# A transformer trunk with two attention branches: the side work of modulation and weight sums goes to GpSimd alone, low parts of weights and masks to VectorE

## The chip, the cores and the metric

The kernel runs on one core of a Trainium2 chip. The core's engines run side by side, each with its own queue of instructions that it works off in order: TensorE (PE in the profile; its weight loads are PEld), VectorE (DVE), ScalarE (ACT), GpSimd (POOL) and SyncE (SP, which here only issues DMAs). An instruction that waits for another engine or for a DMA holds up everything behind it in its own queue, and nothing else. The metric is the device time of one execution in microseconds (us); lower is better. Times of one kernel are given as the median of several runs.

## What is computed

One layer of a streaming encoder on 1024 positions of width 1024, float32 in and out. Cut to what matters:

```python
cond = silu(c)
mod = cond @ w_ada + b_ada                      # six vectors of 1024: shift, scale, gate, twice
sh1, sc1, g1, sh2, sc2, g2 = split(mod, 6)

h = layer_norm(x) * (1 + sc1) + sh1
q_a, k_a, v_a, f_a, q_c, k_c, v_c, gate_a, gate_c = split(h @ w_in)
o_a = forgetting_attention(q_a, k_a, v_a, f_a + b_f)   # causal, 8 heads of 64, cumulative bias
o_c = chunk_band_attention(q_c, k_c, v_c, rel_bias)    # 8 heads, 64-frame chunks, 8 chunks back
merged = sigmoid(gate_a) * (o_a @ w_br_fox) + sigmoid(gate_c) * (o_c @ w_br_chunk)
x = layer_norm(alpha * x + (1 + g1) * (merged @ w_out), ln1_g, ln1_b)

h = layer_norm(x) * (1 + sc2) + sh2
a, val = split(causal_conv3(h @ w_up))
x = layer_norm(alpha * x + (1 + g2) * ((silu(a) * val) @ w_down), ln2_g, ln2_b)
```

## The kernel before

Every matrix product keeps float32 accuracy by splitting its operands: a tile is copied to a rounded high part (`wh`), and the low part (`wl`) is the tile less its high part. Three matmuls (high by high, high by low, low by high) take the place of one. `split` (L100) does this for weights: the copy on ScalarE (L104), the subtraction on GpSimd (L105). A weight tile is 128 x 1024 numbers, loaded into `ws` by `load_w` (L95) through SyncE's queue; `ws`, `wh` and `wl` have two buffers each.

The program has five stretches: the first norm with the first two modulation vectors, attention (from about 113 us), the merge of the branches with the output product, the up-projection with its convolution, and the down-projection. The two large products of the MLP multiply 2 x 2 blocks by a scheme with seven products in place of eight, for which sums and differences of weight blocks are needed; for 8 column blocks of `w_up` and 11 pairs of rows of `w_down` these are prepared during attention and kept in DRAM (`wd`, `td`).

Attention is where the change is. The main loop (L705 to L750) runs over 8 pairs of heads (`plan`), for each over 8 steps of two 128-query blocks. A step computes the scores of the next step (L460, L461 on TensorE), adds the bias and takes the row's extreme on VectorE (L472), the exponential on ScalarE (L478), transposes the probabilities on TensorE (L512), splits them (L515 on ScalarE, L516 on VectorE) and multiplies by the values (L526; added up in L530 and L531). Beside it the loop advances two generators:

- `stream` (class `Stream`): the products of h with `w_in` for later heads and for the gates (tiles `psq`, `psg`, `psv`; L207 to L209 and L309 to L311). It loads raw weights ahead, splits them, and runs units of matmuls. `step` (L263) issues one piece of a unit and then calls `load` and `split`.
- `side_work` (L533): one step of it for each step of `stream` in the loop. It walks through 35 groups, each with one tile `dr` of 128 x 4 x 512 (two buffers). A sums group loads weight blocks, makes four sums or differences on GpSimd (L584) and stores them to `wd` or `td` (L587). A modulation group (16 of them, between the first sums groups) loads half of the rows of 512 columns of `w_ada` (L553), multiplies each of its four 128 x 512 blocks by a column of `cond` on ScalarE (L571) and adds them into `acc` on GpSimd (L573). After two modulation groups TensorE sums `acc` over the partitions (`ada_sums`, L167), and VectorE adds the bias into `modc` (L161, L163).

All loads and stores of the side work go through SyncE's queue, where the loads of weights, of the heads' biases (`cb` for the chunk branch, `fb` for the other) and the copies of queries and keys (`m`, L407, L408) stand as well. GpSimd also writes two masked corners into each `cb` (L425, L426, after VectorE has scaled it, L424) and adds the causal mask to 64 diagonal blocks `fm` (L438).

The order in which instructions stand in each engine's queue is set when the kernel is built: a list scheduler goes over the program with priorities from the order of the code, so that an edit of one engine's work can shift how the two streams interleave on all engines.

Of the kernel before, what the change touches and what calls it, by code (L numbers as in the profile page):

```python
# [12 lines left out]
F32 = mybir.dt.float32  # L13
F32R = mybir.dt.float32r
AF = mybir.ActivationFunctionType
ALU = mybir.AluOpType
# [3 lines left out]
P = 128  # L20
# [4 lines left out]
H = 512  # L25
# [3 lines left out]
DH = 64  # L29
# [3 lines left out]
NEG = -1e30  # L33
# [10 lines left out]
def body(ctx, tc, a, out):  # L44
    nc = tc.nc
    ve, se, pe, po, sy = nc.vector, nc.scalar, nc.tensor, nc.gpsimd, nc.sync
    uid = [0]

    def nm(s):
        uid[0] += 1  # L50
        return f"{s}_{uid[0]}"

    def opened(**kw):
        cm = tc.tile_pool(reuse_waits="tile", **kw)
        return cm, cm.__enter__()
# [8 lines left out]
    def ctile(name, shape, src=None, dt=F32):  # L64
        t = const.tile(shape, dt, name=name, tag=name)
        if src is not None:
            se.dma_start(out=t, in_=src)
        return t
# [10 lines left out]
    cond = ctile("cond", [P, KD])  # L79
# [17 lines left out]
        sy.dma_start(out=st, in_=src)  # L97
        return st

    def split(st, shape, pool=None):  # L100
        n = 2 if pool is None else 1
        hi = (pool or wp).tile(shape, F32R, name=nm("wh"), tag="wh", bufs=n)
        lo = (pool or wp).tile(shape, F32R, name=nm("wl"), tag="wl", bufs=n)
        se.copy(out=hi, in_=st)  # L104
        po.tensor_sub(out=lo, in0=st, in1=hi)  # L105
        return hi, lo

    def split_w(src, shape, pool=None):
# [39 lines left out]
    def ada_src(v, c0, n):  # L148
        return a["w_ada"][:, v * D + c0 : v * D + c0 + n].rearrange("(k p) n -> p k n", p=P)
# [7 lines left out]
    def ada_bias(ps, v, c0, n, plus_one):  # L157
        sl = slice(v * KD + c0 // P, v * KD + (c0 + n) // P)
        ps = ps[:, 0 : n // P]
        if plus_one:  # L160
            ve.scalar_tensor_tensor(out=modc[:, sl], in0=ps, scalar=1.0, in1=bada[:, sl], op0=ALU.add, op1=ALU.add)  # L161
        else:
            ve.tensor_tensor(out=modc[:, sl], in0=ps, in1=bada[:, sl], op=ALU.add)  # L163

    def ada_sums(ps, acc, n):
        for j in range(n // P):
            pe.matmul(ps[:, j : j + 1], acc[:, j * P : (j + 1) * P], ones[:, 0:1], start=True, stop=True)  # L167
# [54 lines left out]
    pmm = es.enter_context(tc.tile_pool(name="pmm", bufs=3, space=PSUM, reuse_waits="tile"))  # L222
# [7 lines left out]
    class Stream:  # L230


        def __init__(self, units):
            self.units = units
            self.parts = [(u, p) for u in range(len(units)) for p in units[u].parts]
            self.loaded, self.ready, self.live, self.age = [], {}, 0, 0
            self.pl = self.ps = self.cur = 0
            self.gen = None

        def load(self):  # L240
            if self.pl < len(self.parts) and self.pl - self.ps < 2:
                _, (src, shape) = self.parts[self.pl]
                self.loaded.append((load_w(src, shape), shape))
                self.pl += 1
                return True
            return False

        def split(self):
            if self.loaded and self.live < 2:
                u = self.parts[self.ps][0]  # L250
                self.ready.setdefault(u, []).append(split(*self.loaded.pop(0)))
                self.ps += 1
                self.live += 1
                return True
            return False
# [7 lines left out]
        def step(self):  # L263
            unit = self.units[self.cur]
            if self.gen is None:
                self.prime(self.cur)
                self.gen = unit.run(self.ready.pop(self.cur, []))
            cost = next(self.gen, None)
            if cost is None:
                self.live -= len(unit.parts)  # L270
                self.gen = None
                self.cur += 1
                cost = 0.0
                self.load()
            else:
                self.load()
                self.split()
            return cost

        def finish(self, upto):  # L280
# [139 lines left out]
    def scaled():  # L420

        while unscaled:
            b = unscaled.pop(0)
            ve.tensor_scalar_mul(b, b, 1.0 / SCALE)  # L424
            po.memset(b[0:DH, 576:640], NEG)  # L425
            po.memset(b[DH:P, 0:64], NEG)  # L426

    def first_block(br, qi):
        return 0 if br == 0 else max(0, qi - 4)
# [3 lines left out]
    def masked(n, i):  # L433

        (ip, hi, g), qi = steps[n], 2 * steps[n][2] + i
        if ip < 4 and (n, i) not in masks:
            fm = ap.tile([P, P], F32, name=nm("fm"), tag="fm", bufs=4)
            po.tensor_tensor(out=fm, in0=heads[ip, hi][3][:, qi * P : (qi + 1) * P], in1=cmask, op=ALU.add)  # L438
            masks[n, i] = fm
        return masks.get((n, i))  # L440

# [91 lines left out]
    def side_work():  # L533

        sub = ALU.subtract
        ups = ((3, 2, 3, ALU.add), (2, 0, 2, sub), (0, 3, 0, sub), (1, 1, 0, sub))
        downs = ((0, 1, 0, sub), (1, 3, 1, sub), (3, 3, 0, sub), (2, 2, 3, sub))
        sums_ = [(ups, a["w_up"][2 * c : 2 * c + 2].rearrange("b p (j k) n -> p b j (k n)", j=2), wd[c]) for c in range(HEAD)]  # L540
        for i in range(NPAIR):
            srcs = [a["w_down"][order[2 * i + r]].rearrange("p (j n) -> p j n", j=2) for r in range(2)]
            sums_.append((downs, srcs, td[i]))
        vecs = [(v, half, q) for v in (2, 4, 3, 5) for half in range(2) for q in range(2)]
        groups = [g for pair in zip(sums_, vecs) for g in pair] + sums_[len(vecs) :]
        tiles, due = {}, []

        def load(n):
            if n < len(groups):
                x = tiles[n] = ap.tile([P, 4, H], F32, name=nm("dr"), tag="dr", bufs=2)  # L550
                if n % 2 and n < 2 * len(vecs):
                    v, half, q = groups[n]
                    sy.dma_start(out=x, in_=ada_src(v, half * H, H)[:, 4 * q : 4 * q + 4, :])  # L553
                else:
                    srcs = groups[n][1]
                    for r in range(2):
                        sy.dma_start(out=x[:, 2 * r : 2 * r + 2, :], in_=srcs[r] if isinstance(srcs, list) else srcs[:, r])

        load(0)
        yield  # L560
        load(1)
        yield
        for n, group in enumerate(groups):
            x = tiles.pop(n)
            if n % 2 and n < 2 * len(vecs):
                v, half, q = group
                if q == 0:
                    acc = ap.tile([P, H], F32, name=nm("acc"), tag="acc", bufs=1)
                for j in range(4):
                    k = 4 * q + j  # L570
                    se.mul(out=x[:, j, :] if k else acc, in_=x[:, j, :], mul=cond[:, k : k + 1])  # L571
                    if k:
                        po.tensor_tensor(out=acc, in0=acc, in1=x[:, j, :], op=ALU.add)  # L573
                    if j % 2:
                        yield
                if q:
                    ps = pmm.tile([P, H], F32, name=nm("psada"), tag="mm")
                    ada_sums(ps, acc, H)
                    due.append(partial(ada_bias, ps, v, half * H, H, v != 3))
            else:  # L580
                while due:
                    due.pop()()
                for j, (o, p, q, op) in enumerate(group[0]):
                    po.tensor_tensor(out=x[:, o, :], in0=x[:, p, :], in1=x[:, q, :], op=op)  # L584
                    if j % 2:
                        yield
                sy.dma_start(out=group[2].rearrange("j p n -> p j n"), in_=x)  # L587
                yield
                yield
            load(n + 2)  # L590
            yield

# [14 lines left out]
    stream = Stream(first_units + [u for grp in groups for u in grp] + [unit_g()])  # L607
# [29 lines left out]
    cmask = ctile("cmask", [P, P], a["cmask"])  # L637
# [8 lines left out]
    for c in range(4):  # L646
# [4 lines left out]
        for v in (0, 1):  # L651
            if v or row is None:
                acc = s1.tile([P, W], F32, name=nm("acc"), tag=f"acc{v}", bufs=1)
# [7 lines left out]
    for kk in range(2):  # L661
        shape = v_unit.parts[kk][1]
        hi = fp.tile(shape, F32R, name=nm("wh"), tag=f"wh{kk}")
        lo = fp.tile(shape, F32R, name=nm("wl"), tag=f"wl{kk}")
# [18 lines left out]
    f_cm.__exit__(None, None, None)  # L683
    ap_cm, ap = opened(name="attn", bufs=2)

    steps = [(ip, i, g) for ip, _ in plan for i in range(2) for g in range(4)]
    heads = {}

# [16 lines left out]
    for u, (ip, _) in enumerate(plan):  # L705
# [5 lines left out]
        for n in range(8 * u, 8 * u + 8):  # L711
            ip, i, g = steps[n]
# [525 lines left out]
    with tc.tile_pool(name="dn", bufs=2, reuse_waits="tile") as dn:  # L1238
# [44 lines left out]
        for p in products:  # L1283
            ps = bank_b if p in ("P5", "P3", "P2") else bank_a
# [44 lines left out]
            elif p in ("P3", "P2", "P7"):  # L1329
                for t in range(4):  # L1330
                    x = {"P3": u2, "P2": p1, "P7": p5}[p][t]
                    ve.tensor_tensor(out=x, in0=ps[t], in1=x, op=ALU.add)
                    tt, n = {"P3": (t, 1), "P2": (t, 0), "P7": (4 + t, 1)}[p]
# [68 lines left out]
```

## Time and profile before

| What | Before |
|---|---|
| Time, median of 3 runs | 1678.43 us (1678.13 to 1678.95) |
| Profiled execution, its time | 1677.85 us |
| Its span on the chip | 1675.7 us |
| TensorE busy | 1544.7 us, 92% |
| VectorE busy | 1029.6 us, 61% |
| ScalarE busy | 788.1 us, 47% |
| GpSimd busy | 594.4 us, 35% |
| DMA of SyncE's queue (q1) | 251.83 MB |
| DMA of ScalarE's queue (q10) | 19.75 MB |
| DMA of GpSimd's queue (q0) | 1.84 MB |

The profile lists what each engine did and when. A row of a waits view reads: engine, tile and line that waited, what it waited for, the total in us, how many times, the longest. A row of a timeline reads: start in us, duration in us, engine, line, operation, written tile and read tiles, shapes; in square brackets how long the engine had been idle before and what ended that. A row of a windows view gives for a stretch its length and the busy time of PE, PEld, DVE, ACT and POOL, then the share of TensorE's clock that was granted (PEclk), the DMA engines' busy share and GB/s. A row of a groups view gives line, engine, operation, tiles, shapes and count, then busy us and mean ns of one, then the idle time before.

### The profile page before, as it was taken

The page shows a single profiled execution, that of the slowest core. Times are in us where ns is not written, and L with a number is a line of the kernel's source. Part 1 is how long each engine was busy: PE and PEld are TensorE (multiplying, and loading weights), DVE is VectorE, ACT ScalarE, POOL GpSimd, SP SyncE. Part 2 cuts the span into 40 slices and gives each one's busy share as a digit, 9 for nine tenths or more (in the row PEclk, how much of TensorE's full clock was granted, in tenths as well). Part 3 has the DMA queues.
Part 4 walks back from the last instruction along what each step waited for, and adds up shares of the span by engine and source line. Part 5 has one row for each costly group of instructions (what it writes and reads, how often), then busy time and mean ns, then how long its engine had stood idle before and what let it go on. Part 6 is the DMA issues. An engine that isn't in the chain of part 4 may idle for free. (4 is left out here: it accounts for less than half of the span.)

```text
span 1675.7 us, 22014 instructions
## 1 busy us (share of the span) xinstructions
PE 1544.7 (92%) x7693; PEld 1293.0 (77%) x7693; DVE 1029.6 (61%) x2053; ACT 788.1 (47%) x1420; POOL 594.4 (35%) x455
## 2 busy tenths in 40 slices
PE   6899788989998799999889798899999999999996
PEld 3788678879777788888667686688888888888885
DVE  6746344445534435443667968667777866855688
ACT  3447444555535434444223435444445455456451
POOL 1126516435355263212303364554544555100000
PEclk9999999999999899999989899899999999999998
DMA  9037735355274354423763725434344222597552
GB/s 358 26 109 252 235 126 177 117 194 183 84 236 153 101 177 157 133 70 111 225 247 118 261 93 197 156 135 149 119 142 166 101 103 86 177 375 251 181 198 81
DMA packets 118766, 274.81 MB, mean 164 GB/s; under 512 B 11008, under 2 KB 19904, under 8 KB 118656
## 3 DMA queue, kind: packets, MB, share of 16 engines
q1 hardware_dynamic: 106464, 251.83, 44.4%
q10 hardware_dynamic: 11664, 19.75, 3.1%
q0 software_dynamic: 528, 1.84, 0.3%
q8 instruction: 60, 0.98, 0.2%
q14 instruction: 50, 0.41, 0.1%
HBM read 197.51 MB, written 67.47 MB: 158 GB/s over the span
## 5 line engine op out<-in xcount | busy, mean ns | idle before, releaser
L105 POOL TENSOR_TENSOR wl<-ws,wh 128x1024 fp32r<-128x1024 f32 x54 | 131.1, 2433 | 312.6 <-ACT wh L104 283.7
L831 PE MATMUL psu<-hc,wx 128*128 128x512 f32 x720 | 168.4, 389 | 0.0
L831 PEld LDWEIGHTS psu<-hc,wx 128*128 128x128 f32 x720 | 135.1, 188 | 28.1
L1067 DVE SCALAR_TENSOR_TENSOR pcv<-u,convp,pcv 128x1024 f32<-128x1024 f32 x88 | 113.2, 1286 | 45.4 <-ACT pcv L1065 44.4
L1208 DVE TENSOR_TENSOR op<-rw,op 128x512 fp32r<-128x512 f32 x146 | 93.3, 688 | 52.9 <-ACT op L1207 52.4
L1207 ACT CAST op<-rw 128x512 fp32r<-128x512 f32 x146 | 85.2, 623 | 83.5 <-PE psd L1220 41.9
L516 DVE TENSOR_TENSOR pt<-pst,pt 128x512 fp32r<-128x512 f32 (+1 forms) x192 | 96.9, 520 | 36.8 <-ACT pt L515 35.3
L478 ACT ACTIVATE s<-s,mx 128x640 f32<-128x640 f32 (+7 forms) x128 | 94.4, 737 | 45.3 <-DVE mx L472 42.9
L584 POOL TENSOR_TENSOR dr<-dr 128x512 f32<-128x512 f32 x76 | 97.9, 1289 | 47.1 <-DMA dr<-in_w_down 21.9
L1219 PE MATMUL psd<-op,op 128*128 128x512 f32 x292 | 113.7, 389 | 0.9 <-DVE op L1208 0.9
L1218 PE MATMUL psd<-op,op 128*128 128x512 f32 x292 | 113.6, 389 | 0.0
L1220 PE MATMUL psd<-op,op 128*128 128x512 f32 x292 | 113.6, 389 | 0.0
L515 ACT CAST pt<-pst 128x512 fp32r<-128x512 f32 (+1 forms) x192 | 82.5, 450 | 56.4 <-PE pst L512 54.6
L526 PE MATMUL pso<-pt,vs 128*128 128x256 f32 x608 | 92.6, 291 | 17.1 <-ACT pt L515 11.6
L207 PE MATMUL psg<-h1h,wh 128*128 128x512 f32 x256 | 107.0, 418 | 0.0
L209 PE MATMUL psq<-h1h,wl 128*128 128x512 f32 x256 | 102.4, 400 | 4.3 <-POOL wl L105 4.3
L209 PE MATMUL psg<-h1h,wl 128*128 128x512 f32 x256 | 102.6, 401 | 4.0 <-POOL wl L105 4.0
L207 PE MATMUL psq<-h1h,wh 128*128 128x512 f32 x256 | 105.8, 414 | 0.4 <-DVE h1h L203 0.4
L208 PE MATMUL psq<-h1l,wh 128*128 128x512 f32 x256 | 102.5, 400 | 1.8 <-DVE h1l L204 1.8
L526 PEld LDWEIGHTS pso<-pt,vs 128*128 128x128 f32 x608 | 83.7, 194 | 26.1 <-ACT pt L515 15.5
L208 PE MATMUL psg<-h1l,wh 128*128 128x512 f32 x256 | 102.4, 400 | 0.0
L512 PE MATMUL pst<-ident,s 128*128 128x128 f32 x528 | 83.2, 277 | 12.6 <-DVE pt L516 9.7
(261 smaller groups left out, 3939.8 us busy)
## 6 DMA issues: line engine op xcount, KB each, us to landing
ws<-in_w_up SPq DMA_DIRECT2D x36, 512.0 KB, 3.7
dr<-in_w_ada SPq DMA_DIRECT2D x16, 1024.0 KB, 5.4
dr<-in_w_down SPq DMA_DIRECT2D x22, 512.0 KB, 4.5
td<-dr SPq DMA_DIRECT2D x11, 1024.0 KB, 4.6
rw<-td SPq DMA_DIRECT2D x44, 256.0 KB, 4.5
yd<-y SPq DMA_DIRECT2D x20, 512.0 KB, 2.8
rw<-yd SPq DMA_DIRECT2D x40, 256.0 KB, 4.0
rw<-sd SPq DMA_DIRECT2D x33, 256.0 KB, 4.7
```

The costliest lines, as they stand in the source:

```text
L105: po.tensor_sub(out=lo, in0=st, in1=hi)
L207: pe.matmul(ps, wh, xh, start=start, stop=False)
L208: pe.matmul(ps, wh, xl, start=False, stop=False)
L209: pe.matmul(ps, wl, xh, start=False, stop=stop)
L516: ve.tensor_sub(out=dl, in0=src, in1=dh)
L526: pe.matmul(ps[:, 0:256], vs[:, h % 2, j0 + j, :], pt[j // 4][:, c, j % 4, :], start=j == 0 and c == 0, stop=j == nj - 1 and c == 1)
L584: po.tensor_tensor(out=x[:, o, :], in0=x[:, p, :], in1=x[:, q, :], op=op)
L831: pe.matmul(ps, w[:, a_, k, :], h[k][b_], start=first, stop=k == 3 and a_ == 1, skip_group_check=on)
L1067: ve.scalar_tensor_tensor(out=ps, in0=u[b][:, 2 - d : S + 2 - d], scalar=cp[:, 2 - d : 3 - d], in1=ps, op0=ALU.mult, op1=ALU.add)
L1218: pe.matmul(ps[t], g[:, 0, ts], d[:, 0], start=start, stop=False, skip_group_check=on)
L1219: pe.matmul(ps[t], g[:, 0, ts], d[:, 1], start=False, stop=False, skip_group_check=on)
L1220: pe.matmul(ps[t], g[:, 1, ts], d[:, 0], start=False, stop=stop, skip_group_check=on)
```

## The change

- In attention the low parts of the stream's weights are subtracted on VectorE (`stream.eng = ve`); before attention and in the merge they stay on GpSimd. The mask additions (L438) and the two corner memsets go to VectorE too.
- In `side_work` the multiplications by `cond` go from ScalarE to GpSimd, and all its loads and stores from SyncE's queue to GpSimd's own.
- `ada_sums` and the bias are issued later: not straight after the second modulation group, but after the store of the sums group that follows it.
- `Stream.step` calls `load` after `split`, so the next raw weight tile is asked for in the same step as the split that frees its buffer.

```diff
-    def split(st, shape, pool=None):
+    def split(st, shape, pool=None, eng=po):
...
-        po.tensor_sub(out=lo, in0=st, in1=hi)
+        eng.tensor_sub(out=lo, in0=st, in1=hi)
...
-                self.ready.setdefault(u, []).append(split(*self.loaded.pop(0)))
+                self.ready.setdefault(u, []).append(split(*self.loaded.pop(0), eng=self.eng))
...
                 cost = 0.0
-                self.load()
             else:
-                self.load()
                 self.split()
+            self.load()
...
-            po.memset(b[0:DH, 576:640], NEG)
-            po.memset(b[DH:P, 0:64], NEG)
+            ve.memset(b[0:DH, 576:640], NEG)
+            ve.memset(b[DH:P, 0:64], NEG)
...
-            po.tensor_tensor(out=fm, in0=heads[ip, hi][3][:, qi * P : (qi + 1) * P], in1=cmask, op=ALU.add)
+            ve.tensor_tensor(out=fm, in0=heads[ip, hi][3][:, qi * P : (qi + 1) * P], in1=cmask, op=ALU.add)
...
-                    sy.dma_start(out=x, in_=ada_src(v, half * H, H)[:, 4 * q : 4 * q + 4, :])
+                    po.dma_start(out=x, in_=ada_src(v, half * H, H)[:, 4 * q : 4 * q + 4, :])
...
-                        sy.dma_start(out=x[:, 2 * r : 2 * r + 2, :], in_=srcs[r] if isinstance(srcs, list) else srcs[:, r])
+                        po.dma_start(out=x[:, 2 * r : 2 * r + 2, :], in_=srcs[r] if isinstance(srcs, list) else srcs[:, r])
...
         load(0)
+        load(1)
         yield
-        load(1)
         yield
...
-                    se.mul(out=x[:, j, :] if k else acc, in_=x[:, j, :], mul=cond[:, k : k + 1])
+                    po.tensor_scalar_mul(x[:, j, :] if k else acc, x[:, j, :], cond[:, k : k + 1])
...
                 if q:
-                    ps = pmm.tile([P, H], F32, name=nm("psada"), tag="mm")
-                    ada_sums(ps, acc, H)
-                    due.append(partial(ada_bias, ps, v, half * H, H, v != 3))
+                    due.append((acc, v, half))
             else:
-                while due:
-                    due.pop()()
...
-                sy.dma_start(out=group[2].rearrange("j p n -> p j n"), in_=x)
+                po.dma_start(out=group[2].rearrange("j p n -> p j n"), in_=x)
                 yield
-                yield
+                while due:
+                    acc, v, half = due.pop()
+                    ps = pmm.tile([P, H], F32, name=nm("psada"), tag="mm")
+                    ada_sums(ps, acc, H)
+                    yield
+                    ada_bias(ps, v, half * H, H, v != 3)
...
+    stream.eng = ve
```

Three places of the engines' queues, before and after; the line numbers of the changed kernel are 1 or 2 higher in parts. The first is ScalarE's queue beside the values' product of a stream unit (`vs` and `psv`), before the change:

```order
L478 ACTIVATE s_2146,sums<-s_2146,mx_2150 128x384
L314 CAST vs_2163<-psv_2165 128x2x64
L571 ACTIVATE dr_2854<-dr_2854,cond 128x512
L314 CAST vs_2164<-psv_2165 128x2x64
L515 CAST pt_2145<-pst_2203 128x2x128
L571 ACTIVATE dr_2854<-dr_2854,cond 128x512
L478 ACTIVATE s_2196,sums<-s_2196,mx_2200 128x512
```

and the same place of the changed kernel, where the same tiles have other numbers:

```order
L478 ACTIVATE s_2150,sums<-s_2150,mx_2154 128x384
L314 CAST vs_2170<-psv_2172 128x2x64
L515 CAST pt_2149<-pst_2214 128x2x128
L314 CAST vs_2171<-psv_2172 128x2x64
L478 ACTIVATE s_2207,sums<-s_2207,mx_2211 128x512
```

The multiplications of `dr` (L571) are gone from between the copies that attention and the stream wait for. The second place is VectorE's queue at the evacuation of a stream product (`qm` from `psq`), before:

```order
L472 ISA s_1965,mx_1969<-pss_1966,cb_1550 128x384
L472 ISA mx_1969 128x1
L368 TENSOR_TENSOR qm_1789<-psq_1890,qm_1789 64x512
L472 ISA s_1965,mx_1974<-pss_1971,cb_1550,mx_1969 128x256
L472 ISA mx_1974 128x1
```

and in the changed kernel:

```order
L472 ISA s_1973,mx_1977<-pss_1974,cb_1553 128x384
L472 ISA mx_1977 128x1
L105 TENSOR_TENSOR wl_2015<-ws_1646,wh_2014 128x1024
L368 TENSOR_TENSOR qm_1786<-psq_1893,qm_1786 64x512
L472 ISA s_1973,mx_1982<-pss_1979,cb_1553,mx_1977 128x256
L472 ISA mx_1982 128x1
```

A low part now stands between the two halves of a score row. The third place is GpSimd's queue around two modulation groups (`dr_2276` and `dr_2739`) and the sums group between them (`dr_2561`), in the changed kernel alone:

```order
L583 DMA wd<-dr_2130 128x4x512
L571 TENSOR_SCALAR dr_2276<-dr_2276,cond 128x512 x3
L557 DMA dr_2561<-in_w_up 128x1024 x2
L580 TENSOR_TENSOR dr_2561<-dr_2561 128x512 x4
L583 DMA wd<-dr_2561 128x4x512
L553 DMA dr_2739<-in_w_ada 128x4x512
L571 TENSOR_SCALAR dr_2739<-dr_2739,cond 128x512 x4
L571 TENSOR_SCALAR acc_2612<-dr_2276,cond 128x512
L573 TENSOR_TENSOR acc_2612<-acc_2612,dr_2276 128x512 x3
L557 DMA dr_2882<-in_w_up 128x1024 x2
L573 TENSOR_TENSOR acc_2612<-acc_2612,dr_2739 128x512 x4
```

GpSimd's queue in this stretch holds side work alone, each load just ahead of the instructions that use it.

More of the change, by code (lines that the diff above doesn't have):

```diff
@@ L235, in __init__ @@
             self.parts = [(u, p) for u in range(len(units)) for p in units[u].parts]
-            self.loaded, self.ready, self.live, self.age = [], {}, 0, 0
+            self.loaded, self.ready, self.live = [], {}, 0
+            self.eng = po
             self.pl = self.ps = self.cur = 0
```

## The prediction

> **What bounds the kernel now.** I read the windows view first, because the change touches attention alone. Two stretches of it, with the columns PE, PEld, DVE, ACT, POOL, PEclk:
>
> ```profile
> 113.00:620.00 507.00, 453.45 (x2664) 399.18 (x2663) 232.54 (x708) 260.59 (x586) 238.53 (x203) 0.95 0.52 171
> 620.00:770.00 150.00, 150.00 (x827) 129.12 (x827) 74.24 (x229) 73.01 (x154) 42.20 (x44) 1.00 0.38 127
> ```
>
> The end of attention runs without a hole and at full clock: TensorE alone bounds it, although the splits and masks go on there. Up to 620 us, with the side work beside it, TensorE is idle for 507.00 - 453.45 = 53.6 us and gets 0.95 of its clock, which is 25 us of full clock not granted. So at most 79 us lie here. Next the waits of TensorE in attention, which account for nearly all the idle time (53.3 us):
>
> ```profile
> PE pso L526 <- ACT pt L515: 11.6, 4, 5.6
> PE pst L512 <- DVE pt L516: 9.7, 3, 5.6
> PE psv L309 <- ACT wh L104: 8.1, 1, 8.1
> PE pss L460 <- DVE mx L472: 5.6, 4, 3.1
> PE pso L526 <- DVE pt L516: 5.4, 3, 3.0
> PE psq L209 <- POOL wl L105: 4.3, 1, 4.3
> PE psg L209 <- POOL wl L105: 4.0, 1, 4.0
> PE pst L512 <- ACT s L478: 2.7, 1, 2.7
> PE psv L310 <- POOL wl L105: 1.9, 2, 1.5
> ```
>
> The view names the last link only. The timeline of one wait shows what lies behind it (TensorE, ScalarE, then two later matmuls):
>
> ```profile
> 230.73 0.58 PE L526 MATMUL pso<-pt,vs 128*128 128x256 f32 x1 [5.39 <-ACT pt L515]
> 229.53 0.72 ACT L571 ACTIVATE dr<-dr,cond 128x512 f32<-128x512 f32 x1 [5.56 <-DMA dr<-in_w_ada]
> 230.30 0.37 ACT L515 CAST pt<-pst 128x256 fp32r<-128x256 f32 x1
> 231.32 0.41 PE L309 MATMUL psv<-wh,h1h 128*128 128x256 f32 x1
> 554.38 0.28 PE L309 MATMUL psv<-wh,h1h 128*128 128x256 f32 x1
> ```
>
> A copy of probabilities stood in ScalarE's queue behind a multiplication of the side work that waited for its load, and TensorE waited with it. After the wait the same matmul takes 0.41 us, where it takes 0.28 us elsewhere: a long wait is paid for again in clock. ScalarE waited for these loads 12 times (an idle time that ended with "issue" before L571 is the same, with its wait in ScalarE's sequencer):
>
> ```profile
> ACT dr L571 <- DMA dr<-in_w_ada: 41.8, 8, 9.5
> ACT dr L571 <- issue: 23.4, 4, 10.9
> 503.84 0.43 DVE L531 TENSOR_TENSOR o<-pso,ot 64x256 f32<-64x256 f32 x1 [6.38 <-ACT ot L530]
> 424.44 0.43 DVE L531 TENSOR_TENSOR o<-pso,ot 64x256 f32<-64x256 f32 x1 [4.45 <-ACT ot L530]
> ```
>
> The two VectorE rows are waits that began on ScalarE and reached TensorE under VectorE's name (3.1 us of the 5.6 before L460, 2.1 of the 9.7 before L512). The third cause is SyncE's queue:
>
> ```profile
> SPq L97 <- POOL wl L105: 162.2, 28, 20.3
> SPq L587 <- POOL dr L584: 71.6, 16, 5.5
> 332.77 0.33 SPq L97 DMA_DIRECT2D ws<-in_w_v  x1
> 333.75 0.54 SPq L414 DMA_DIRECT2D cb<-in_rel_t  x1
> 339.91 0.49 DVE L424 TENSOR_SCALAR cb<-cb 128x640 f32<-128x640 f32 x1 [6.99 <-DMA cb<-in_rel_t]
> 174.83 0.49 DVE L424 TENSOR_SCALAR cb<-cb 128x640 f32<-128x640 f32 x1 [7.31 <-DMA cb<-in_rel_t]
> ```
>
> The bias load stood behind a weight load that waited for a low part, which stood on GpSimd behind side work. VectorE stood still for it, and TensorE after it (5.6 us of L512's and 3.0 of L526's waits).
>
> **The change part by part.** *ScalarE's multiplications go.* TensorE's waits named ACT, 11.6 + 8.1 + 2.7 = 22.4 us, and the 5.2 us that came by way of VectorE: 27.6 us. ScalarE also loses 64 x 0.72 = 46 us of work. *Low parts leave GpSimd.* There they waited behind sums; TensorE waited 4.3 + 4.0 + 1.9 = 10.2 us. *SyncE's queue loses the side work*, and the low part frees the weight buffer sooner: 8.6 us of bias waits. I count all of it, though one later bias load, issued as soon as its buffer was free, will still come late. `load` after `split` I cost at nothing, since no wait of TensorE above leads back to a raw weight tile. Together 46.4 of 53.3 us; of the other 6.9 us I count nothing.
>
> *The clock.* Of the 25 us not granted some fall on idle time. In the quoted wait 5 us of matmuls went at about half pace, after a wait of 5.4; I take 18 us for the whole stretch, and of it the share 46.4/53.3, 15.7 us. Removed in all: **62 us**.
>
> *What VectorE gets.* The rows for its price:
>
> ```profile
> L105 POOL TENSOR_TENSOR wl<-ws,wh 128x1024 fp32r<-128x1024 f32 x54 | 131.1, 2433 | 312.6 <-ACT wh L104 283.7
> L116 DVE TENSOR_TENSOR wl<-ws,wh 128x1024 fp32r<-128x1024 f32 x12 | 14.7, 1222 | 7.5 <-ACT wh L115 7.4
> L315 DVE TENSOR_TENSOR vs<-psv,vs 128x128 fp32r<-128x128 f32 x48 | 13.9, 290 | 48.7 <-ACT vs L314 48.5
> L817 DVE TENSOR_TENSOR wt<-ws,s 128x512 f32<-128x512 f32 x14 | 18.5, 1325 | 2.2 <-POOL wx L820 1.2 <-POOL wh L820 0.6
> L1208 DVE TENSOR_TENSOR op<-rw,op 128x512 fp32r<-128x512 f32 x146 | 93.3, 688 | 52.9 <-ACT op L1207 52.4
> ```
>
> 35 low parts x 1.22 + 64 masks x 0.29 (the row of that size) = 61 us, on an engine that is busy 232.54 of 507 us. Both operands of a low part and of a mask lie in SBUF, and such an instruction is slower beside GpSimd: L817 stands beside GpSimd's low parts and takes 1.33 us, L1208 of the same size has GpSimd idle and takes 0.69. With 0.6 us for each of 99 instructions and GpSimd busy for 0.58 of the time (below), 34 us more: 95 us. The Trainium skill (SBUF — State Buffer, section "Who interferes with whom") speaks against this part of the change: a VectorE instruction with two SBUF inputs and a GpSimd instruction that reads SBUF exclude each other for the whole of the one that came first. By it the 99 could each lose a whole GpSimd instruction of 1.29 us, 74 us in place of my 34; the two rows agree with the rule in kind, at half that size.
>
> How much of 95 us reaches TensorE is not shown. Below: nothing, as between 620 and 770 us, where VectorE is busy for 49% and TensorE never waits. Above: the share that reached it from ScalarE's waits, 27.6 of 65.2 us or 0.42, that is 40 us, and with clock in the same proportion as above (15.7 to 46.4) 54 us. The nearest row is the same subtraction in the same place on GpSimd: 34 of them at 2.4 us made 82 us, of which TensorE waited 10.2, or 0.12. I take **12 us**.
>
> *What GpSimd gets.*
>
> ```profile
> L584 POOL TENSOR_TENSOR dr<-dr 128x512 f32<-128x512 f32 x76 | 97.9, 1289 | 47.1 <-DMA dr<-in_w_down 21.9
> L573 POOL TENSOR_TENSOR acc<-acc,dr 128x512 f32<-128x512 f32 x56 | 72.4, 1293 | 56.3 <-ACT acc L571 47.8 <-ACT dr L571 5.2
> L1094 POOL DMA_DIRECT2D sd<-sc x3 | 1.8, 592 | 22.5 <-DVE sc L1087 22.1 <-issue 0.4
> dr<-in_w_ada SPq DMA_DIRECT2D x16, 1024.0 KB, 5.4
> L1091 POOL DMA_DIRECT2D yd<-y x1 | 0.5, 531 | 0.2 <-issue 0.2
> L167 PE MATMUL psada<-ones,acc x64: 164/250/250, 168.3 to 655.2; 128*128 128x1 f32 x64
> ```
>
> It loses 82 us of low parts. The 64 multiplications have no row on GpSimd: between 0.72 us (ScalarE's) and 1.29 (GpSimd's sum of that size, which reads twice as much); I take 1.29. A DMA issue there takes 0.59 us for 128 rows of 2 KB and 0.53 for 128 of 4 KB; the loads of `w_ada` and the stores have 512 rows, so up to 2.4 if rows count, and 0.59 if not, which I take. With 73 issues: 97.9 + 72.4 + 82.6 + 43 = 296 us of the 507. It hides behind TensorE as long as `acc` is done when `ada_sums` comes. That happens 8 times in 168 to 655 us, every 69 us; in the changed order the first and the last stand 5% fewer stream matmuls apart, and with the gain that leaves 59 us. Two pairs of groups cost GpSimd (8 + 7 + 8) x 1.29 + 8 x 0.59 = 34 us, and three loads that stand just ahead of their use, at 5.4 us or a little more, 17 us: 51 of 59. With four issues at 2.4 it is 58. So the cover holds, thinly at the upper end; I take **0**, and price its failure below.
>
> **The sum**, against the profiled execution's 1677.85 us (span 1675.7 and 2.15 around it; 0.6 under the median): 1677.85 - 62 + 12 = **1628 us**.
>
> **The rivals.** *GpSimd is late.* If the issues with 512 rows cost 2.4 us and GpSimd loses the same 34 us to VectorE as VectorE to it, two pairs take 58 + 4 = 62 us: 3 us late 8 times, 24 us, with clock 32: 1660. For it: no row shows such an issue. Against: twice the bytes made no dearer issue in the rows above.
>
> *The queue buys only issue time.* Then bias loads come as late as before, and 8.6 us and 2.9 of clock stay: 1639. The Trainium skill (DMA: Bandwidth & Descriptors, section "Issuing engines are not separate DMA queues") says that issuing from several engines saves only the sequencer's time. Against it stand the waits in SyncE's queue above, which are order, not bandwidth.
>
> *VectorE inherits GpSimd's wait* (the slower side). A low part needs ScalarE's copy first:
>
> ```profile
> POOL wl L105 <- ACT wh L104: 107.0, 18, 21.2
> ```
>
> If VectorE stands still for all of that, in the middle of a score row, 0.42 of it reaches TensorE, with clock 0.56: 60 us, and with the 12 above 1688. It decides from 50/0.56 = 89 us, 2.5 us for each split. Against: GpSimd came early because its queue was empty; VectorE arrives with work of the same step, and ScalarE's own stops before the copy go.
>
> *The change of order gives it back.* The two streams interleave anew on TensorE; new waits of the old size: 1678, no change.
>
> **How the numbers follow.** Forecast 0.64; GpSimd late 0.08; issue time only 0.08; order 0.07; VectorE's wait 0.13. Low end: all 53.3 us and 18 of clock gone, nothing new: 1607. High end: VectorE's upper bound, 1678 - 62 + 54 = 1670, which takes in the late GpSimd. Left out is about 0.2. Faster by over 0.2% (3.4 us, about what a measurement can tell from no change) 0.80, within it 0.07, slower 0.13.
>
> **What would show it.** Between 113 and 600 us the idle time of TensorE falls from 53.6 to under 20 us and PEclk rises to 0.98 or more; ScalarE has no L571 row; VectorE's L424 waits shrink from 22.0 us; VectorE is busy some 60%; `psada` rows show no wait for GpSimd. Wrong if TensorE waits for VectorE's `wl` or `acc` by more than 20 us, or if L105 on VectorE takes over 2 us.

## The result, and the profile after

The changed kernel takes 1629.41 us (median of 4 runs, 1620.54 to 1633.05) beside 1678.28 us of the kernel before on the same chip: a ratio of 0.9702, 95% interval 0.9662 to 0.9741. The forecast of 1628.0 us stands within 1.4 us of it, closer than the runs lie to one another. The sum was right and its terms were not, as the experiments show. The profiled execution took 1633.05 us, the slowest of the four, with a span of 1631.3.

First the windows view of the side work's stretch (length, then busy PE, PEld, DVE, ACT, POOL, granted clock, DMA share, GB/s), before and after:

```profile
113.00:600.00 487.00, 437.44 (x2595) 386.05 (x2594) 227.90 (x694) 255.54 (x575) 224.36 (x193) 0.95 0.52 169
```

```profile
113.00:600.00 487.00, 465.06 (x2811) 412.09 (x2810) 301.39 (x843) 236.69 (x552) 316.75 (x260) 0.98 0.55 182
```

TensorE's idle time fell from 49.6 to 21.9 us and its clock rose from 0.95 to 0.98, so it did 8% more matmuls in the same stretch. All of the gain lies here: the same places of the merge behind attention come 43 to 46 us earlier, and the end 44.4. TensorE's waits in that stretch after the change:

```profile
PE psada L167 <- POOL acc L573: 11.0, 2, 8.8
PE pss L460 <- DVE mx L472: 5.6, 5, 3.8
PE pst L512 <- DVE pt L516: 4.5, 5, 1.7
PE pso L526 <- DVE pt L516: 0.6, 1, 0.6
```

Every wait for ScalarE and for GpSimd's `wl` is gone. A new one is the largest: the sums over `acc` (L167) wait for GpSimd's last addition. The timeline of the longer wait (GpSimd, then TensorE):

```profile
513.85 1.26 POOL L580 TENSOR_TENSOR dr<-dr 128x512 f32<-128x512 f32 x1 [1.75 <-DMA dr<-in_w_down]
...
518.85 1.26 POOL L573 TENSOR_TENSOR acc<-acc,dr 128x512 f32<-128x512 f32 x1
...
520.16 1.87 PE L167 MATMUL psada<-ones,acc 128*128 128x1 f32 x8 [8.76 <-POOL acc L573]
521.89 3.76 PE L526 MATMUL pso<-pt,vs 128*128 128x256 f32 x16
```

GpSimd is still at the additions, mixed with the next group's sums and their load, when TensorE arrives. Behind the wait, 16 matmuls take 3.76 us, 0.235 each; the matmuls of this width ahead of it followed one another in 0.12. GpSimd's groups of instructions (busy us, mean ns of one, idle time before):

```profile
L580 POOL TENSOR_TENSOR dr<-dr 128x512 f32<-128x512 f32 x71 | 94.0, 1325 | 58.7 <-DMA dr<-in_w_down 32.8 <-DMA dr<-in_w_up 23.0
L571 POOL TENSOR_SCALAR dr<-dr,cond 128x512 f32<-128x512 f32 x56 | 89.7, 1613 | 43.6 <-DMA dr<-in_w_ada 43.2
L573 POOL TENSOR_TENSOR acc<-acc,dr 128x512 f32<-128x512 f32 x56 | 77.0, 1374 | 2.5
L557 POOL DMA_DIRECT2D dr<-in_w_down x22 | 12.6, 573 | 4.6 <-DMA td<-dr 2.8 <-POOL acc L573 1.6 <-issue 0.2
L553 POOL DMA_DIRECT2D dr<-in_w_ada x15 | 11.8, 785 | 33.5 <-DMA td<-dr 18.2 <-DMA wd<-dr 14.4 <-POOL acc L573 0.8
L583 POOL DMA_DIRECT2D wd<-dr x8 | 6.5, 814 | 7.3 <-issue 5.2 <-POOL dr L580 2.1
```

The multiplication costs 1.61 us, more than the addition that reads twice as much (1.37). An issue costs 0.57 us for 128 rows and 0.79 to 0.81 for 512. GpSimd also stands 32.6 us before a load (L553), because the buffer's store must have landed first, and 21.1 us before its own stores, a wait for which the profile names no cause. On VectorE:

```profile
L105 DVE TENSOR_TENSOR wl<-ws,wh 128x1024 fp32r<-128x1024 f32 x27 | 38.3, 1418 | 27.8 <-ACT wh L104 27.7
L438 DVE TENSOR_TENSOR fm<-fb,cmask 128x128 f32<-128x128 f32 x44 | 19.2, 443 | 6.8 <-DMA fb<-fd 3.3 <-DMA rd<-rt 3.2
L424 DVE TENSOR_SCALAR cb<-cb 128x640 f32<-128x640 f32 x8 | 6.1, 767 | 11.2 <-DMA cb<-in_rel_t 11.2
```

VectorE is busy for 301.39 of 487 us, 62%. It waits 27.7 us for ScalarE's copies, where GpSimd waited 86.8 in the same stretch, and for bias rows 11.2, where it was 22.0.

### The profile page after: what moved, and what is told of

Same layout as the page of the kernel before. It is cut to its first block, busy times and chain, and to the rows that moved or that the text cites. A ratio compares the mean times of both kernels' runs of the same rounds, so it can differ in the third digit from the quotient of the medians.

```text
span 1631.3 us, 21827 instructions
## 1 busy us (share of the span) xinstructions
PE 1529.6 (94%) x7693; PEld 1283.6 (79%) x7693; DVE 1096.5 (67%) x2168; ACT 750.1 (46%) x1356; POOL 638.7 (39%) x477
## 5 line engine op out<-in xcount | busy, mean ns | idle before, releaser
L105 POOL TENSOR_TENSOR wl<-ws,wh 128x1024 fp32r<-128x1024 f32 x19 | 48.3, 2548 | 283.0 <-ACT wh L104 280.3
L1069 DVE SCALAR_TENSOR_TENSOR pcv<-u,convp,pcv 128x1024 f32<-128x1024 f32 x88 | 113.1, 1286 | 45.4 <-ACT pcv L1067 44.4
L478 ACT ACTIVATE s<-s,mx 128x640 f32<-128x640 f32 (+7 forms) x128 | 94.4, 738 | 57.9 <-DVE mx L472 56.0
L571 POOL TENSOR_SCALAR dr<-dr,cond 128x512 f32<-128x512 f32 x56 | 89.7, 1613 | 43.6 <-DMA dr<-in_w_ada 43.2
L104 ACT CAST wh<-ws 128x1024 fp32r<-128x1024 f32 x54 | 56.3, 1047 | 78.3 <-PE psq L208 27.5
```

The lines of the kernel that those rows point to most:

```text
L478: se.activation(out=st[:, 0:nk], in_=st[:, 0:nk], func=AF.Exp, scale=-1.0, bias=prev, accum_out=sums[:, col : col + 1])
L1069: ve.scalar_tensor_tensor(out=ps, in0=u[b][:, 2 - d : S + 2 - d], scalar=cp[:, 2 - d : 3 - d], in1=ps, op0=ALU.mult, op1=ALU.add)
```

## The experiments

All times are medians; the kernel before took 1677.25 to 1679.5 us beside each set.

### Undoing one part of the change at a time

Multiplications back on ScalarE:

```diff
-                    po.tensor_scalar_mul(x[:, j, :] if k else acc, x[:, j, :], cond[:, k : k + 1])
+                    se.mul(out=x[:, j, :] if k else acc, in_=x[:, j, :], mul=cond[:, k : k + 1])
```

> The changed kernel with its 64 multiplications of the modulation back on ScalarE; all else as changed. Forecast's theory (ScalarE standing behind the loads of dr was the main loss): ScalarE waits for dr again, the exponentials and copies behind it come late, TensorE loses about 28 us of waits and some 9 us of clock as before the change, less about 11 us of waits and 7 us of clock that GpSimd's lateness costs now, since GpSimd is 103 us of work lighter: about 1648 us (1640 to 1665). Rival (the queue was what counted: on GpSimd's own queue the dr loads come early, so ScalarE hardly waits): 1612 to 1630 us, and multiplications are no part of the gain.

Measured: 1718.43 us, ratio to the kernel before 1.024 (1.0216 to 1.0264), 89 us over the changed kernel. Both theories missed, the rival even in direction. The waits of GpSimd and of ScalarE:

```profile
POOL acc L573 <- ACT acc L571: 138.5, 6, 31.9
...
ACT dr L571 <- DMA dr<-in_w_ada: 110.3, 14, 11.7
```

GpSimd now issues the loads of `dr`, in order behind additions that wait for ScalarE's products, while ScalarE's products wait for those loads. ScalarE's wait for `dr` was 65.2 us in the kernel before; here it is 110.3, and TensorE waits 27.5 us for ScalarE's copies. So the queue on GpSimd is good only if the multiplications are there too.

Low parts back on GpSimd:

```diff
-    stream.eng = ve
+    stream.eng = po
```

> The changed kernel with the 34 low parts of the attention's weights back on GpSimd, so that VectorE computes none of them. Forecast's theory (GpSimd is in order and short of time): 34 low parts of 1.4 to 2.4 us are 47 to 82 us more on an engine that is busy for 317 of 487 us, each behind a wait for ScalarE's copy; low parts come late (10 us of waits of TensorE and clock) and the weight sums later than the 11 us they cost now: 1650 to 1680 us. Rival (the low parts' engine does not matter, or VectorE's 47 us cost TensorE as much): 1620 to 1633 us.

Measured: 1724.33 us, ratio 1.0288 (1.0264 to 1.0313). The direction was expected, but the loss of 95 us is larger than the range. Three of TensorE's waits:

```profile
PE psv L310 <- POOL wl L105: 41.2, 4, 18.1
...
PE psq L209 <- POOL wl L105: 16.0, 2, 10.9
PE psg L209 <- POOL wl L105: 5.6, 1, 5.6
```

They make 62.8 us, where it was 6.2 in the same stretch of the kernel before: a low part now stands behind products, issues and waits for `dr`.

Side loads and stores back on SyncE's queue (L557 and L583 like L553):

```diff
-                    po.dma_start(out=x, in_=ada_src(v, half * H, H)[:, 4 * q : 4 * q + 4, :])
+                    sy.dma_start(out=x, in_=ada_src(v, half * H, H)[:, 4 * q : 4 * q + 4, :])
```

> The changed kernel with the loads and stores of the side work back on SyncE's queue, multiplications still on GpSimd. Forecast's theory (SyncE's queue stands behind loads of dr that wait for a free buffer, so bias loads and weights come late): 9 to 12 us of waits for VectorE's bias rows return, and the clock with them: 1640 to 1655 us. Rival (a queue of its own saves only the time of issuing): GpSimd is freed of 73 issues of 0.57 to 0.81 us, some 50 us, and is less late at the sums: 1612 to 1630 us.

Measured: 1654.31 us, ratio 0.9857 (0.9837 to 0.9878), 25 us over the changed kernel: the forecast's theory, and not the rival. VectorE's wait for bias rows and two waits of SyncE's queue say why:

```profile
DVE cb L424 <- DMA cb<-in_rel_t: 43.9, 5, 14.0
...
SPq L583 <- POOL dr L580: 93.3, 19, 5.8
SPq L557 <- POOL acc L573: 86.7, 10, 18.1
```

SyncE stands before a store or a load that waits for GpSimd, with the bias loads behind it. `psada` no longer waits here: TensorE comes to the eight sums 11 to 37 us later than in the changed kernel, and GpSimd, which issues no loads and stores, is done with the last four 4 to 20 us earlier.

Mask additions and fills back on GpSimd (L425 and L426 like L438):

```diff
-            ve.tensor_tensor(out=fm, in0=heads[ip, hi][3][:, qi * P : (qi + 1) * P], in1=cmask, op=ALU.add)
+            po.tensor_tensor(out=fm, in0=heads[ip, hi][3][:, qi * P : (qi + 1) * P], in1=cmask, op=ALU.add)
```

> The changed kernel with the 64 mask additions and 16 fills of the bias back on GpSimd. Forecast's theory (masks on VectorE cost little there, 64 times 0.39 us; on GpSimd each waits in order for its bias and for buffers): 28 us more of work and the order's waits on GpSimd make its sums later: 1632 to 1650 us. Rival (VectorE's new load is what holds the gain down): 25 us less on VectorE give 3 to 15 us back: 1614 to 1626 us.

Measured: 1688.28 us, ratio 1.0068 (1.0045 to 1.0091): 59 us over the changed kernel, slower than before the change and beyond both ranges. VectorE's new load of 64 masks is far from being what holds the gain down; without it the gain is gone. The wait of VectorE's score rows, then TensorE's:

```profile
DVE s L472 <- POOL fm L438: 61.7, 8, 40.7
...
PE pss L460 <- DVE mx L472: 49.2, 3, 38.9
```

A mask that takes 0.5 us on GpSimd came up to 40.7 us late.

### Building the change up from the kernel before

The first half alone, low parts, masks and fills on VectorE:

```diff
+    stream.eng = ve
...
-            po.tensor_tensor(out=fm, in0=heads[ip, hi][3][:, qi * P : (qi + 1) * P], in1=cmask, op=ALU.add)
+            ve.tensor_tensor(out=fm, in0=heads[ip, hi][3][:, qi * P : (qi + 1) * P], in1=cmask, op=ALU.add)
```

> The kernel before with one half of the change alone: low parts, mask additions and fills go to VectorE; the multiplications stay on ScalarE and the side loads on SyncE's queue. Forecast's theory (ScalarE behind dr and the shared queue are the larger loss): only the 10 us of waits for GpSimd's low parts and a few us of clock go, 1678 to 1655-1670 us. Rival drawn from the first four runs (short, urgent work in GpSimd's order was the block; undoing it cost 59 and 95 us): this half brings most of the gain, 1630 to 1648 us.

Measured: 1662.18 us, ratio 0.9904 (0.988 to 0.9927): 17 us gained, as the forecast's theory has it. Beside the waits for `wl`, part of ScalarE's wait for `dr` went as well, from 65.2 us to 25.7 and 17.7:

```profile
ACT dr L572 <- DMA dr<-in_w_ada: 25.7, 6, 5.5
ACT dr L572 <- issue: 17.7, 6, 7.8
```

The other half alone, multiplications on GpSimd and side work on its queue (all three DMA lines), in the old order of the code:

```diff
-                    se.mul(out=x[:, j, :] if k else acc, in_=x[:, j, :], mul=cond[:, k : k + 1])
+                    po.tensor_scalar_mul(x[:, j, :] if k else acc, x[:, j, :], cond[:, k : k + 1])
...
-                sy.dma_start(out=group[2].rearrange("j p n -> p j n"), in_=x)
+                po.dma_start(out=group[2].rearrange("j p n -> p j n"), in_=x)
```

> The kernel before with the other half alone: multiplications on GpSimd, side loads and stores on its queue; low parts, masks and fills stay on GpSimd too, old order of the code. If the two halves add up (the offload alone gave 17 us, both together in the old order 64): 1678 minus 47, some 1631 us. If the halves need each other (GpSimd takes its work in order, so masks and low parts stand behind multiplications, issues and waits for dr, and VectorE and TensorE wait for them): slower than before, 1690 to 1740 us, with VectorE's waits for fm over 60 us or TensorE's for GpSimd's wl over 40 us.

Measured: 1719.0 us, ratio 1.0251 (1.0228 to 1.0274), 42 us slower. The halves do not add up: they need each other. TensorE's two largest waits here:

```profile
PE psq L209 <- POOL wl L105: 30.3, 3, 16.7
PE psv L310 <- POOL wl L105: 26.5, 4, 16.0
```

The first half with the multiplications on GpSimd, loads still on SyncE's queue:

```diff
+    stream.eng = ve
...
-                    se.mul(out=x[:, j, :] if k else acc, in_=x[:, j, :], mul=cond[:, k : k + 1])
+                    po.tensor_scalar_mul(x[:, j, :] if k else acc, x[:, j, :], cond[:, k : k + 1])
```

> The half above, and the multiplications on GpSimd too; loads still on SyncE's queue, order of the code as before. Forecast's theory: ScalarE's 27.6 us of waits and the clock go, the queue's 9 to 12 us stay: 1640 to 1655 us. Rival (only the whole package works: sums early in the old order now wait for GpSimd's slower products at every one of eight places, 5 to 9 us each): 1670 to 1700 us.

Measured: 1643.03 us, ratio 0.9792 (0.9765 to 0.9818): 19 us more gained. The rival's waits did not come. VectorE waits for bias rows longer than before, though, and SyncE, which loads them, for GpSimd:

```profile
DVE cb L425 <- DMA cb<-in_rel_t: 39.4, 5, 12.8
...
SPq L558 <- POOL acc L574: 94.4, 9, 27.6
```

All moves between engines and queues, in the old order of the code, shown against the changed kernel at two of its places:

```diff
-            self.load()
+                self.load()
...
-                    due.append((acc, v, half))
+                    ps = pmm.tile([P, H], F32, name=nm("psada"), tag="mm")
+                    ada_sums(ps, acc, H)
+                    due.append(partial(ada_bias, ps, v, half * H, H, v != 3))
```

> All moves between engines and queues, in the old order of the code: the sums are issued as soon as their group ends, weights are loaded after the split of a unit's end, and the second side load stands one step later. If the order of the code is worth nothing: 1625 to 1635 us, like the changed kernel. If it is needed, because TensorE reaches the sums while GpSimd is still at the products: 1645 to 1680 us, with waits of psada for acc of 30 us and more.

Measured: 1615.27 us, ratio 0.962 (0.9597 to 0.9642). This is faster than the changed kernel by 14 us, which neither side expected. Its stretch has no wait for `psada` and the full clock:

```profile
113.00:600.00 487.00, 476.96 (x2894) 421.95 (x2893) 313.06 (x862) 242.35 (x565) 325.51 (x262) 1.00 0.56 186
```

So the queue's move is worth 28 us here, and the edits of the code's order cost 14.

### Why the new order costs 14 us

The sums moved half a group later, behind the next group's four products, with that group's first addition after them:

```diff
-                    po.tensor_scalar_mul(x[:, j, :] if k else acc, x[:, j, :], cond[:, k : k + 1])
+                    po.tensor_scalar_mul(x[:, j, :], x[:, j, :], cond[:, k : k + 1])
...
+                if q == 0:
+                    yield from folded()
+                    acc = ap.tile([P, H], F32, name=nm("acc"), tag="acc", bufs=1)
+                    for j in range(1, 4):
+                        po.tensor_tensor(out=acc, in0=acc if j > 1 else x[:, 0, :], in1=x[:, j, :], op=ALU.add)
```

`folded` holds the lines from `ada_sums` to `ada_bias`.

> The changed kernel with the eight sums issued about half a group later, behind the next group's four products, whose first sum is written only after that (as many instructions as before). Theory (GpSimd's lateness at the sums costs 11 us of waits and some 7 us of clock): 1612 to 1622 us, with no wait of psada for GpSimd. Rival (the lateness moves on: GpSimd's next sum waits for TensorE to read the old one, and all behind it comes later): 1627 to 1645 us.

Measured: 1622.51 us, ratio 0.9665 (0.9643 to 0.9686), between the two ranges and a little faster than the changed kernel; the intervals overlap. The wait moved to the last of the eight sums:

```profile
PE psada L167 <- POOL acc L579: 11.6, 1, 11.6
```

A later place postpones the end of the cover; the cover still shrinks from sum to sum. From the trace rows of `psada` and of the last addition before it, the time between them, in us, for the eight sums:

| Kernel | Cover of `acc` before the sums 1 to 8 |
|---|---|
| changed | 30.1, 25.7, 22.2, 12.0, 4.7, 0.0, 0.1, 13.7 |
| all moves, old order | 20.2, 26.3, 30.2, 28.8, 33.1, 22.8, 21.7, 21.7 |
| sums half a group later | 43.6, 38.8, 27.9, 18.3, 16.0, 5.9, 2.8, 0.1 |

The old code takes 5 steps for a sums group and 3 for a modulation group, 16 for two of each. The new order drops the empty step of one sums group and puts the weight sums into that of the other: 15. Each step stands beside a piece of the projections. So by the eighth sum TensorE has done 1872 projection matmuls in the changed kernel and 1920 in the old order, though by the first it had done 492 against 468.

An empty step put back in every second sums group of the changed kernel:

```diff
+                if not due:
+                    yield
                 while due:
                     acc, v, half = due.pop()
```

> The changed kernel with one empty step more in every second group of weight sums, so that four groups take 16 steps beside the projections, as in the old code, and not 15; all else as changed. Pace theory (the shorter step list brings TensorE to the sums 72 projection matmuls earlier by the eighth sum than the old list does, faster than GpSimd works; the cover of 30 us at the first sum is gone at the sixth): 1613 to 1621 us, no wait of psada for acc, 20 us or more between GpSimd's last addition and each sum. Rival (the other edits of the order cost the 14 us, the waits at psada being only where it shows): 1625 to 1635 us.

Measured: 1613.55 us, ratio 0.9632 (0.9605 to 0.9658), just below the changed kernel's interval. No `psada` wait is left; the covers run 39.3, 38.0, 30.6, 25.6, 20.6, 21.6, 15.5, 10.0. TensorE's idle time in the stretch is 7.5 us, at full clock:

```profile
113.00:600.00 487.00, 479.46 (x2920) 425.71 (x2920) 311.14 (x873) 245.20 (x571) 311.25 (x251) 1.00 0.55 181
```

One empty step thus wins the loss back. That it would keep 20 us of cover at each sum was too much.

The other edit of the order, `load` after `split`, undone in the changed kernel:

```diff
+                self.load()
             else:
+                self.load()
                 self.split()
-            self.load()
```

> The changed kernel with the weights' next load issued ahead of the split again, and after a unit's end without a split, as before the change; pace of the side work as changed. Pace theory: the two waits at psada stay, 1624 to 1634 us. Rival (load after split makes weights late and costs the 14 us): 1612 to 1621 us.

Measured: 1628.15 us, ratio 0.9698 (0.9665 to 0.9732), the same as the changed kernel. TensorE waits 10.5 us at `psada`. The pace theory holds: the run with the empty step, measured beside this one, is 14.6 us faster.

Each multiplication written with two inputs:

```diff
-                    po.tensor_scalar_mul(x[:, j, :] if k else acc, x[:, j, :], cond[:, k : k + 1])
+                    po.tensor_tensor(out=x[:, j, :] if k else acc, in0=x[:, j, :], in1=cond[:, k : k + 1].to_broadcast([P, H]), op=ALU.mult)
```

> The changed kernel with each multiplication on GpSimd written as a two-input multiplication by the column repeated along the row, in place of a scalar operand; same order on TensorE, VectorE, ScalarE and SyncE. Theory (the scalar form costs GpSimd 1.61 us, a two-input form 1.32 to 1.37 us; that excess, 64 times 0.27, is what makes it late): 2.1 us less per group, the waits at psada shrink from 11.0 to 0 to 3 us and 1614 to 1623 us. Rival (a multiplication costs the same in either form, or the repeated operand more): GpSimd 1.6 us each, 1626 to 1640 us.

Measured: 1631.21 us (five runs, 1620.98 to 1638.39), ratio 0.9707 (0.9672 to 0.9742). The multiplication fell to 1.07 us, below either theory, and `psada` no longer waits (covers of 23.5 us and more); the time did not follow, and lies in the rival's range for another reason than the rival's. GpSimd's group and two of VectorE's in the profiled run:

```profile
L571 POOL TENSOR_TENSOR dr<-dr,cond 128x512 f32<-128x512 f32 x56 | 58.3, 1066 | 44.0 <-DMA dr<-in_w_ada 43.8
...
L105 DVE TENSOR_TENSOR wl<-ws,wh 128x1024 fp32r<-128x1024 f32 x27 | 44.7, 1657 | 29.3 <-ACT wh L104 29.1
L438 DVE TENSOR_TENSOR fm<-fb,cmask 128x128 f32<-128x128 f32 x45 | 28.5, 640 | 4.7 <-DMA fb<-fd 4.1 <-DMA rd<-rt 0.3
```

VectorE's timeline where a bias row is scaled (start, duration):

```profile
138.68 2.96 DVE L424 TENSOR_SCALAR cb<-cb 128x640 f32<-128x640 f32 x1
141.56 0.41 DVE L516 TENSOR_TENSOR pt<-pst,pt 128x256 fp32r<-128x256 f32 x1
```

VectorE's low parts and masks became slower than in the changed kernel, by 0.24 and 0.20 us each. The scaling, 0.49 us where GpSimd is idle, took 2.96 us while GpSimd went from an addition to a multiplication to two issues without a pause, and TensorE's waits for VectorE rose from 10.7 to 17.1 us. The slower VectorE is a likely reason that the time did not follow; no run isolates it. The profiled run took 1622.58 us; the spread of the five leaves open whether anything was gained.

## Why the prediction was right

TensorE's waits for ScalarE and for GpSimd's `wl`, which the prediction named, did go. That the total is right to 1.4 us is luck: four errors of 14 to 18 us, two of each sign, nearly cancel. The terms, in the order before, first half, multiplications, queue, code order, each predicted term of waits with its share of the clock (62.1/46.4):

| Term of the sum | Predicted | Measured |
|---|---|---|
| Low parts and masks to VectorE: -10.2 x 1.34 + 12 | -1.7 | -17.3 |
| Multiplications off ScalarE: -27.6 x 1.34 | -36.9 | -19.2 |
| Side work off SyncE's queue: -8.6 x 1.34 | -11.5 | -27.8 |
| Order of the code and GpSimd's lateness | 0 | +14.1 |
| Sum | -50.1 | -50.1 |

The last measured term is the difference of medians from two sets, in which the kernel before took 1678.28 and 1679.50 us. The column holds for this order alone: the last three terms cannot stand first, since multiplications and queue without the first half cost 42 us. The prediction treated the waits as separate terms; they are links of queues that wait for one another.

- *ScalarE's multiplications: right mechanism, too large alone.* The waits for ScalarE are gone and its L571 row with them. But a third of ScalarE's wait for `dr`, 65.2 us before and 43.4 with the first half alone, went with the low parts. An explanation is at hand: loads of `dr` stood in SyncE's queue behind weight loads that waited for GpSimd's `wl`. SyncE's waits fit it (98.5 us behind `wl` on GpSimd before, 35.1 behind `wl` on VectorE with the first half alone), and no run isolates it.
- *Low parts and masks: mis-sized.* I priced VectorE's load at 12 us and found nothing for the masks' departure. With the multiplications on GpSimd, masks left there cost 59 us and low parts 95. So these moves do not merely pay for the others, they make them possible.
- *VectorE's own price.* Predicted were 61 us of work and 34 beside GpSimd. Over attention, 34 low parts took 46.9 us and 64 masks 24.6, together 71.5; at 1.22 and 0.29 they would have taken 60.0, so 11.5 us came from GpSimd beside them. Of the 12 us that I let reach TensorE little shows: its waits that end with VectorE make 10.7 us in the stretch, and 6.9 us of such waits had been left standing in the forecast. The Trainium skill (SBUF — State Buffer, section "Who interferes with whom") describes an exclusive lock; the traces agree in kind, by the rows of the two-input experiment, and its extreme of 74 us did not come in the changed kernel. The rival in which VectorE inherits a wait of 107.0 us fell: over the whole of attention it waits 32.1.
- *SyncE's queue: mis-sized by more than half.* Bias rows were only the visible part. With multiplications on GpSimd, SyncE waits for GpSimd before loads and stores of the side work (94.4 us for L558 and 90.4 for L588 in the run without the queue's move), and the bias rows' wait grows from 20.8 to 39.4 us. The Trainium skill (DMA: Bandwidth & Descriptors, section "Issuing engines are not separate DMA queues") promises the issue time only; two pairs of runs show 25 and 28 us from the queue, with the bytes unchanged. What went is not issue time but standing still: the bias rows and weights in SyncE's queue no longer stand behind side loads and stores that wait for GpSimd.
- *GpSimd's cover: the step that failed.* I set 51 us of need against 59 between sums and took 0. In the changed kernel the first six sums stand 56.4 us apart on average ((459.9 - 178.1)/5), and the cover falls by 30.1 us over them, 6.0 each, so the need was 62.4. Of it 38.6 is work (8 x 1.61 + 7 x 1.37 + 8 x 1.32 and 5.5 for eight issues; I had 34), and the rest, 23.8 us where I had 17, is waiting for loads and, unforeseen, ahead of stores and for them to leave the buffer. The rival of a late GpSimd came true, not by dear issues but by dear multiplications, these waits and a pace of 15 steps for 16. It cost 14 us by the old order, 16 by the slower pace, and not 32.
- *The clock.* Granted TensorE clock in the stretch rose from 0.95 to 0.98, about 15 us of 487, as forecast (15.7). The wait of 8.76 us before the seventh sum was paid for in clock too: half clock set in at 513.78 us, inside the wait, and held for 13.65 us. In the old order and with the empty step, where no `psada` wait is left, the clock is 1.00.
- *What was to show it.* VectorE's 62%, the bias waits, the clock and L105 at 1.42 us came as written. TensorE's idle time is 21.9 us and not under 20 (from 49.6; the 53.6 of the prediction belongs to the stretch up to 620 us), and `psada` does wait. That was the sign of the 14 us that a slower pace returns.

## What to carry to other kernels

Before a slow, load-bound job is given to an in-order engine, take the short urgent work off it: the two halves of this change were worth -17 and +42 us alone and -64 together. Where such a job feeds another engine at fixed places of a program, compare how fast it works with how fast the places come, place by place; a cover of 30 us at the first was gone at the sixth. Put such a job's loads on the queue of the engine that uses the data (25 and 28 us here), and keep the whole chain of the job there, or two in-order queues wait for each other (89 us here).

## What the hardware showed unexpectedly

On GpSimd, multiplying 128 x 512 numbers by a scalar column took 1.61 us, the same with the column repeated as a second input 1.07, and an addition 1.32 to 1.40. On VectorE, in the changed kernel, the subtraction of 128 x 1024 took 1.22 us with GpSimd idle, 1.38 beside GpSimd's scalar form and 1.69 beside its two-input form (means of the 9 and 6 instructions that lay at least 70% beside it); a mask took 0.27, 0.40 and 0.78. VectorE's instructions that read a product from PSUM did not change (L368: 0.69 us in all cases). Runs of the changed kernel scatter by 0.8%, those of the kernel before by 0.1% in the same set and up to 0.6% in the others; why was not settled.
